# Two token groups with one gathered and one dense block in each, first gathers issued with the second mixer, and U products in four-pass float32

## The chip, the cores and the metric

The kernel runs on one core of a Trainium2 chip. The metric is the device time of one execution in microseconds, the median over executions. The core has five instruction streams that run side by side, each in its own order: TensorE (PE, with its weight loads PEld), VectorE (DVE), ScalarE (ACT), GpSimd (POOL) and SyncE (SP). SP issues the plain table loads, POOL the indirect ones, ACT some stores; the transfers themselves are carried by 16 DMA engines.

## The reference

One decoder block over 512 tokens of 1,024 features, float32, with 16 learned meta tokens in front. A mixer with two branches (8 heads of stick-breaking attention, 4 heads of gated linear attention) comes first, then a layer of 16,384 single-neuron experts. Each token looks up 128 of them, 16 for each of 8 heads, by the largest sums of two key scores:

```python
    s1 = jnp.einsum('thd,hkd->thk', q[:, :, 0], sub_keys1).astype(jnp.float32)
    s2 = jnp.einsum('thd,hkd->thk', q[:, :, 1], sub_keys2).astype(jnp.float32)
    v1, i1 = lax.top_k(s1, PEER_TOPK)
    v2, i2 = lax.top_k(s2, PEER_TOPK)
    cand = (v1[..., :, None] + v2[..., None, :]).reshape(T, PEER_HEADS, PEER_TOPK * PEER_TOPK)
```

The layer's output for a token is the sum over its 128 experts of softmax gate x gelu(x . U[e]) x V[e], where U and V are tables of 16,384 rows of 1,024 values (64 MiB each). It is added to the residual, and a last norm follows.

## The kernel before

The 512 tokens are four blocks of 128. `GROUPS = ((0, 1, 2), (3,))` makes two token groups. `front(g)` runs both mixer branches for a group (the second attends to the keys and values of the first too), `mid(g)` the output projection, the residual, the second norm and the expert queries. `proj` streams weights in chunks of 256 columns and multiplies them with the group's tokens, in one of two ways: *split*, where `hilo` makes a high and a low part of each operand and `mm3` (lines 185 to 189) multiplies three pairs of parts in one pass each; or *native*, one float32 product that the engine works off in four passes (two instructions in the trace). `topk(blk)` is a block's lookup, on VectorE almost alone: first the key scores, then the 16 largest, then tables.

Blocks in `DENSE` (0, 1, 2) compute **all** experts densely. For each of 128 groups of 128 experts (first key i1), `u_phase(i1)` loads a tile `uf` of the U table, splits it on ACT and VectorE (`uh`, `ul`) and makes 24 split passes of 384 token columns; gelu goes into a ring of 24 tiles. `v_operands(i1)` loads `vf`, splits it, and multiplies the ring tile with the dense weights `gt`; `v_block` adds 18 passes of 512 columns into six PSUM banks. `LA` = 23: U runs 23 groups ahead of V. The dense weights come from `spread(blk)`: for four tokens at a time it forms two one-hot operands (`B` on VectorE, `Am` on GpSimd, line 861), multiplies them (`px`, line 865) and stores the result to `Gd` in DRAM.

The block in `GATHER` (3) fetches its own rows. `gather` (line 807) is an indirect DMA on GpSimd's queue: one row of U or V for each of 128 tokens, 512 KB, into one of `GB` = 5 buffers `gu`. `u_dot` makes a dot product with it on VectorE (line 814, x in `xn`), `v_sum` adds a weighted V row to `y` (line 825), in a fixed order. So 128 + 128 gathers and as many VectorE operations serve a block.

The order of all this is the order in which Python issues it, refined by a scheduler that keeps each engine's queue in order. `SCHED` is a list written by hand for the second group: pieces of its mixer (f), middle (m), lookups (t, c) and spreads (s) of blocks 0 to 2 between them, and three early U products. Block 3's lookup and its gathers go into the dense stage, `TRATE` and `GRATE` steps per expert group.

Of the kernel before, what the change touches and what calls it, by code (L numbers as in the profile page):

```python
# [31 lines left out]
# PSUM banks for the key scores of the four blocks  # L32
SCT = ("px", "pz", "pz", "px")
# [30 lines left out]
NATIVE_PQ = (False, True)  # L64


def build(tc, d, out):
# [14 lines left out]

    wp = pool_open("wts", "wts0", side="right")
# [4 lines left out]
    # PSUM banks: 8 = pj 2, pz 3, po 3 (first group); pj 2, pk 2, pz 2, px 2 (second group); pj 2, acc 6  # L88
    nbuf = dict(pz=3, po=3)
# [17 lines left out]
    Gd = drp.tile([TB, 128, 128, TT], F32, name="Gd")  # L107
    hd = drp.tile([4, 128, D], F32, name="hd")

# [26 lines left out]
    def consts_b():  # L136
        nc.sync.dma_start(wgu, d["wgu"])
        nc.sync.dma_start(bgu, d["bgu"])
        lvf = pp.tile([128, 8, 128], F32, name="kT0")
# [19 lines left out]
    def rstd(ss, n, np_, pool, tag):  # L159
        """(ss / D + eps) ** -0.5 of sums of squares [np_, n]: exp(-ln / 2) and one Newton step."""  # L160
# [68 lines left out]
    def front(g):  # L229
        """Both mixer branches for the query blocks of group g; the meta tokens go with group 0."""  # L230
# [8 lines left out]
        oTh = (pp if g == 0 else wp).tile([128, KT, W], F32 if nato else F32R, name=f"oT{g}h")  # L239
        oTl = None if nato else pp.tile([128, KT, W], F32R, name=f"oT{g}l")  # L240
# [4 lines left out]
        kT = (pp if g == 0 else ap).tile([128, 4, W], F32, name=f"kT{g}")  # L245
        vt = (pp if g == 0 else ap).tile([128, nb, 512], F32, name=f"v{g}")
# [14 lines left out]
        def columns(x, rows, col, q):  # L261
            """A quarter of the features of normalised rows as columns of hn."""
# [26 lines left out]
        def rows_(c, vtile, mtile):  # L289
            """A chunk of values: tokens on partitions."""  # L290
            banks, outs, jobs = token_jobs(nb, NM, pm_)
            if g == 0:
                pm = banks[-1][:66, 256:]
                jobs.append((pm, 't', 0, 256, 0, 66, False))
# [25 lines left out]
        def gla_scores():  # L320
# [59 lines left out]
            for l in range(8):  # L380
                level(l)

        def gla_values():
            for c in range(2):
                cs = slice(c * 256, (c + 1) * 256)
                rows_(8 + c, gv[:, :, cs], gvm[:, cs] if g == 0 else None)

        def gla_out():
# [34 lines left out]
            for b, blk in enumerate(blks):  # L423
# [11 lines left out]
                if blk < 3:  # L435
                    state(NM + b * 128, 128, gv[:, b], False)

        def gla_silu():
            for c in range(2):
                for m, p in enumerate(feat(10 + c, NM)):  # L440
# [4 lines left out]
                    V.tensor_tensor(gr[:, 2 * c + m], p, e, op=OP.mult)  # L445

        def gla_norm():
            np_ = 2 if 2 * W <= 512 else 1
            n = np_ * W
            for s in range(2):  # L450
                for pr0 in range(0, 2, np_):
# [7 lines left out]
                    for j in range(np_):  # L459
# [6 lines left out]
                        else:  # L466
                            V.tensor_mul(rr[:, c_], rr[:, c_], gr[:, hh])
                            hilo(oTh[:, 4 + hh], oTl[:, 4 + hh], rr[:, c_])

        def sb_proj():  # L470
# [652 lines left out]
```

## Time and profile before

| what | value |
|---|---|
| three runs | 1712.67, 1713.15, 1717.16 us; median 1713.15 |
| profiled execution | span 1712.3 us |
| busy, share of the span | PE 95%, DVE 72%, ACT 41%, POOL 31% |
| DMA | 376.04 MB, mean 220 GB/s over the span |
| chain that ended last, by engine | PE 77%, DVE 14%, DMA 4%, ACT 2% |

The profiled execution's span is the stretch from its first to its last instruction; the runs are timed around it. A busy share is a mean over stages with different limits: the program runs through the first mixer group, lookups and second mixer, then the dense stage.

### The profile page before, as it was taken

How to read it: one execution, taken by the hardware profiler on the slowest of the kernel's cores; microseconds unless marked ns; L12 is line 12 of the kernel's file. 1: busy time of each engine (PE TensorE's matmuls, PEld its weight loads, DVE VectorE, ACT ScalarE, POOL GpSimd, SP SyncE). 2: the span in 40 equal slices, each digit the busy share in tenths (PEclk: the TensorE clock that was granted, in tenths of full speed). 3: DMA queues.
4: the chain of work that ended last, by engine and by line, in shares of the span. 5: the costliest groups of instructions: out<-in, count | busy, mean ns of one | idle time of the engine just before them, and what ended most of it. 6: DMA issues, size and time to landing. Idle time of an engine off the chain costs nothing.

```text
span 1712.3 us, 24535 instructions
## 1 busy us (share of the span) xinstructions
PE 1625.8 (95%) x9025; PEld 1448.6 (85%) x9025; DVE 1230.3 (72%) x2484; ACT 703.9 (41%) x1104; POOL 529.2 (31%) x401
## 2 busy tenths in 40 slices
PE   6999998988888799999999999999999999999996
PEld 5967988976678788989999999999999999999885
DVE  4225737389989998988777777777777777777674
ACT  5357355324455566333333333333333333333343
POOL 0020000002455565045434344343344443434310
PEclk9989999999999899999999999999999999999998
DMA  5210215243254345689887887887888887877653
GB/s 173 82 38 28 96 63 191 82 153 111 99 195 187 136 177 214 201 271 375 322 301 280 301 320 281 315 299 277 309 304 295 303 302 293 307 278 281 213 200 134
DMA packets 145705, 376.04 MB, mean 220 GB/s; under 512 B 13712, under 2 KB 63008, under 8 KB 142512
## 3 DMA queue, kind: packets, MB, share of 16 engines
q1 hardware_dynamic: 104112, 211.92, 36.2%
q0 software_dynamic: 36864, 134.23, 21.2%
q10 hardware_dynamic: 4608, 28.31, 4.1%
q8 instruction: 71, 1.16, 0.3%
q14 instruction: 50, 0.41, 0.1%
HBM read 345.03 MB, written 29.36 MB: 219 GB/s over the span
## 4 chain that ended last, share of the span: by engine, by line
PE 77%; DVE 14%; DMA 4%; ACT 2%; issue 1%; POOL 1%; SPq 0%; DVEq 0%; ACTq 0%; POOLq 0%
PE pj L189 12%; PE pj L187 12%; PE pj L188 12%; PE acc L188 9%; PE acc L189 9%; PE acc L187 9%; PE pk L209 3%; DVE B L859 2%; PE px L865 2%; PE pz L522 1%; PE pz L373 1%; PE pz L530 1%; DVE sc L775 1%; DMA gu<-expert_u,idx 1%; DMA vf<-expert_v 1%
## 5 line engine op out<-in xcount | busy, mean ns | idle before, releaser
L189 PE MATMUL pj<-xDh,ul 128*128 128x384 f32 x1000 | 337.3, 337 | 2.5 <-DVE ul L183 2.5
L187 PE MATMUL pj<-xDh,uh 128*128 128x384 f32 x1000 | 336.6, 337 | 0.0
L188 PE MATMUL pj<-xDl,uh 128*128 128x384 f32 x1000 | 336.2, 336 | 0.0
L188 PE MATMUL acc<-vl,wh 128*128 128x512 f32 x762 | 298.8, 392 | 2.8 <-DVE vl L183 2.8
L189 PE MATMUL acc<-vh,wl 128*128 128x512 f32 x762 | 298.6, 392 | 0.0
L187 PE MATMUL acc<-vh,wh 128*128 128x512 f32 x762 | 296.2, 389 | 0.0
L807 POOL DMA_INDIRECT gu<-expert_u,idx x128 | 189.4, 1479 | 324.2 <-DVE gu L814 183.7
L807 POOL DMA_INDIRECT gu<-expert_v,idx x128 | 178.7, 1396 | 277.2 <-DVE y L825 201.5
L182 ACT ACTIVATE uh<-uf 128x1024 fp32r<-128x1024 f32 x125 | 132.5, 1060 | 304.0 <-PE pj L188 262.4
L183 DVE TENSOR_TENSOR ul<-uf,uh 128x1024 fp32r<-128x1024 f32 x125 | 157.3, 1258 | 56.1 <-ACT uh L182 56.1
L187 PEld LDWEIGHTS pj<-xDh,uh 128*128 128x128 f32 x1000 | 188.3, 188 | 4.2
L188 PEld LDWEIGHTS pj<-xDl,uh 128*128 128x128 f32 x1000 | 188.2, 188 | 4.0
L189 PEld LDWEIGHTS pj<-xDh,ul 128*128 128x128 f32 x1000 | 188.2, 188 | 3.9 <-DVE ul L183 3.5
L188 PEld LDWEIGHTS acc<-vl,wh 128*128 128x128 f32 x762 | 143.0, 188 | 32.2 <-DVE vl L183 4.3
L189 PEld LDWEIGHTS acc<-vh,wl 128*128 128x128 f32 x762 | 143.0, 188 | 29.8
L187 PEld LDWEIGHTS acc<-vh,wh 128*128 128x128 f32 x762 | 143.1, 188 | 27.8 <-ACT vh L182 0.4
L825 DVE SCALAR_TENSOR_TENSOR y<-gu,act,y 128x1024 f32<-128x1024 f32 x128 | 163.9, 1280 | 0.5
L183 DVE TENSOR_TENSOR vl<-vf,vh 128x1024 fp32r<-128x1024 f32 x127 | 155.1, 1221 | 10.2 <-ACT vh L182 10.2
L861 POOL TENSOR_TENSOR Am<-ohu,ohl 128x512 f32<-128x512 f32 x96 | 132.6, 1399 | 95.3 <-PE px L865 57.8
L814 DVE SCALAR_TENSOR_TENSOR gu<-gu,xn 128x1024 f32<-128x1024 f32 x128 | 154.7, 1219 | 8.1 <-DMA gu<-expert_u,idx 8.1
L182 ACT ACTIVATE vh<-vf 128x1024 fp32r<-128x1024 f32 x127 | 133.0, 1047 | 16.7 <-DMA vf<-expert_v 14.4
L865 PE MATMUL px<-Am,B 128*128 128x128 f32 x768 | 105.5, 289 | 24.8 <-DVE B L859 13.2
(365 smaller groups left out, 2507.9 us busy)
## 6 DMA issues: line engine op xcount, KB each, us to landing
vf<-expert_v SPq DMA_DIRECT2D x128, 512.0 KB, 3.7
uf<-expert_ut SPq DMA_DIRECT2D x125, 512.0 KB, 5.0
wf<-w_in SPq DMA_DIRECT2D x48, 512.0 KB, 3.7
Gd<-st ACTq DMA_DIRECT2D x24, 1024.0 KB, 4.0
gt<-Gd SPq DMA_DIRECT2D x16, 1536.0 KB, 12.4
wf<-w_out SPq DMA_DIRECT2D x16, 512.0 KB, 3.7
wf<-w_pq SPq DMA_DIRECT2D x16, 512.0 KB, 3.7
h<-x SPq DMA_DIRECT2D x4, 512.0 KB, 6.5
```

The source lines that it names most:

```text
L182: A.activation(hi, src, AF.Copy)
L183: V.tensor_tensor(lo, src, hi.bitcast(F32), op=OP.subtract)
L187: T.matmul(outp, lh, rh, start=first, stop=False, skip_group_check=True)
L188: T.matmul(outp, lh, rl, start=False, stop=False, skip_group_check=True)
L189: T.matmul(outp, ll, rh, start=False, stop=last, skip_group_check=True)
L209: T.matmul(o, l, r, start=st, stop=sp, skip_group_check=True)
L807: P.indirect_dma_start(out=u, out_offset=None, in_=d[table], in_offset=bass.IndirectOffsetOnAxis(ap=col, axis=0))
L814: V.scalar_tensor_tensor(u, u, 1.0, xns[blk], op0=OP.mult, op1=OP.mult, accum_out=acts[blk][:, k:k + 1]))
L825: V.scalar_tensor_tensor(y, u, acts[blk][:, k:k + 1], y, op0=OP.mult, op1=OP.add))
L859: V.tensor_tensor(B, io4, iT[:, 1, c_].unsqueeze(2).to_broadcast(sh), op=OP.is_equal)
L861: P.tensor_tensor(Am.rearrange("p t (u l) -> p t u l", l=8), ohu[:, l_].unsqueeze(3).to_broadcast([128, 4, 16, 8]), ohl[:, l_].unsqueeze(2 ...
L865: T.matmul(p[:, j * 128:(j + 1) * 128], B[:, j], Am[:, j], start=True, stop=True)
```

## The change

The token groups become two of two blocks. In each the first block (0, 2) gathers and the second (1, 3) runs densely, so 512 gathers are issued instead of 256, and each dense product has 256 token columns instead of 384. Expert groups are taken in 64 pairs: one PSUM bank holds both groups' U results. U products are native float32 straight from the loaded tile `uf`, with no split; V products are native in every second pair (`V_NATIVE`) and split in the others. `Gd` has another layout (runs of 512 B in its writes, 8 KB in its reads).

The hand-written list goes. Every piece is now a generator that yields its estimated cost, and `weave(main, rate)` issues `rate` times that cost in background steps after each piece of a main sequence. The background has two queues: `look` (lookups and spreads) and `rows` (the gathered blocks' steps); `MIX` weighs them. The lookup of block 0 is issued whole right after the second group's first norm; then come `front(1)` and `mid(1)` with block 0's first gathers and the lookup of block 1; then 19 U pairs ahead of V with the lookup of block 3 and both spreads; then the dense loop with the lookup of block 2 and the other gathers; what is left is issued behind it. The core of the diff, without the many `yield` lines added to the mixer pieces:

```diff
+SCT = ("pz", "px", "px", "px")
...
-GROUPS = ((0, 1, 2), (3,))
-DENSE = (0, 1, 2)
-GATHER = (3,)
+GROUPS = ((0, 1), (2, 3))
+DENSE = (1, 3)
+GATHER = (0, 2)
 ND = len(DENSE)
+DT = ND * 128
 TT = 16
-TB = ND * 128 // TT
+TB = DT // TT
 IC = 8
-# float32 products as four passes (True) or as three passes over operands split in two (False), per token group
+NPAIR = NK // 2
...
+V_NATIVE = lambda p: p % 2 == 1
+RATES = (0.75, 1.0, 0.55)
+MIX = 0.4
+LA = 19
...
-    Gd = drp.tile([TB, 128, 128, TT], F32, name="Gd")
+    Gd = drp.tile([NK // IC, 128, TB, TT * IC], F32, name="Gd")
...
-            st = bp.tile([128, 128, TT], F32, name="st", bufs=2)
+            st = bp.tile([128, NK // IC, TT, IC], F32, name="st", bufs=2)
...
+            nc.scalar.dma_start(Gd[:, :, 128 // TT * DENSE.index(blk) + tb].rearrange("g p x -> p g x"),
+                                st.rearrange("p g t l -> p g (t l)"))
...
+    def gathered(blk):
+        for k in range(NK):
+            u_dot(blk, k)
+            yield 1.3
+        weights(blk, slice(0, NK))
+        y = gb.tile([128, D], F32, name=f"y{blk}")
+        ys[blk] = y
+        nc.sync.dma_start(y, hd[blk])
+        for k in range(NK):
+            v_sum(blk, y, k)
+            yield 1.3
...
+    def step(queue):
+        while queue:
+            c = next(queue[0], None)
+            if c is not None:
+                return c
+            queue.pop(0)
+        return None
+    mixed = [0.0]
+    def background():
+        if look and (not rows or mixed[0] < 1.0):
+            c = step(look)
+            if c is not None:
+                mixed[0] += MIX
+                return c
+        mixed[0] -= 1.0
+        return step(rows)
+    owed = [0.0]
+    def weave(main, rate):
+        for cost in main:
+            owed[0] += cost * rate
+            while owed[0] > 0:
+                c = background()
+                if c is None:
+                    owed[0] = 0.0
+                    break
+                owed[0] -= c
+    def finish(queue):
+        while step(queue) is not None:
+            pass
...
+    tks = {b: topk(b) for b in range(4)}
+    next(tks[0])
     pool_close("wts")
-    mp = pool_open("mid", "mid", side="right")
+    pool_close("ps")
+    gb = ctx.enter_context(tc.tile_pool(name="gat", bufs=1, reuse_waits="tile"))
+    wp = pool_open("wts", "wts1", side="right")
+    ps = pool_open("ps", "psb1", space=PSUM)
+    f1 = front(1)
+    next(f1)
+    for _ in range(1000):
+        if next(tks[0], None) is None:
+            break
+    rows.append(gathered(0))
+    look.append(tks[1])
+    weave(f1, RATES[0])
+    weave(mid(1), RATES[0])
+    finish(look)
...
+    def u_pair(p_):
+        ge = ring[p_] = du.tile([128, 2, DT], F32, name="ge", bufs=LA + 1)
+        pu = pj()
+        for i in range(2):
             uf = du.tile([128, KT, 128], F32, name="uf", bufs=2)
...
+            nc.sync.dma_start(uf, d["expert_ut"][2 * p_ + i])
+            for kt in range(KT):
+                T.matmul(pu[:, i * DT:(i + 1) * DT], uf[:, kt], xg[:, kt, :, 1, :], start=kt == 0, stop=kt == KT - 1)
+        A.activation(ge.rearrange("p a t -> p (a t)"), pu, AF.Gelu)
+    def ahead(n):
+        for p_ in range(n):
+            u_pair(p_)
+            yield 7.0
+    look.extend([tks[3], spread(1, 3), spread(3, 3)])
+    weave(ahead(LA), RATES[1])
+    finish(look)
+    look.append(tks[2])
...
+    def v_operands(p_):
         nonlocal gt
...
+        ge = ring.pop(p_)
+        vs = []
+        for i in range(2):
+            vf = dp.tile([128, D], F32, name="vf", bufs=3)
+            nc.sync.dma_start(vf, d["expert_v"][(2 * p_ + i) * 128:(2 * p_ + i + 1) * 128, :])
+            vs.append(vf)
+        if 2 * p_ % IC == 0:
+            gt = dp.tile([128, DT, IC], F32, name="gt", bufs=2)
+            nc.sync.dma_start(gt.rearrange("p t l -> p (t l)"), Gd[2 * p_ // IC].rearrange("p a x -> p (a x)"))
+        o = 2 * p_ % IC
+        V.tensor_tensor(ge, ge, gt[:, :, o:o + 2].rearrange("p t l -> p l t"), op=OP.mult)
+        if V_NATIVE(p_):
+            return ge, vs
+        wh = dp.tile([128, 2, DT], F32R, name="wh", bufs=2)
+        wl = dp.tile([128, 2, DT], F32R, name="wl", bufs=2)
+        hilo(wh, wl, ge)
+        hl = []
+        for vf in vs:
             vh = dp.tile([128, D], F32R, name="vh", bufs=2)
             vl = dp.tile([128, D], F32R, name="vl", bufs=2)
...
+            hilo(vh, vl, vf)
+            hl.append((vh, vl))
+        return (wh, wl), hl
+    def v_pair(p_, ops, ijs):
+        w, vs = ops
+        for e in range(2):
+            first, last = p_ == 0 and e == 0, p_ == NPAIR - 1 and e == 1
+            for i, j in ijs:
+                ts, ds_ = slice(i * 128, (i + 1) * 128), slice(j * 512, (j + 1) * 512)
+                if V_NATIVE(p_):
+                    T.matmul(acc[i][j], w[:, e, ts], vs[e][:, ds_], start=first, stop=last, skip_group_check=True)
+                else:
+                    mm3(acc[i][j], (w[0][:, e, ts], w[1][:, e, ts]), (vs[e][0][:, ds_], vs[e][1][:, ds_]), first, last)
+    ALL = [(i, j) for i in range(ND) for j in range(2)]
+    def dense():
+        started = False
+        for p_ in range(NPAIR):
+            if p_ + LA < NPAIR:
+                u_pair(p_ + LA)
+            ops = v_operands(p_)
+            if p_ < NPAIR - 1:
+                v_pair(p_, ops, ALL)
+            else:
+                for ij in ALL:
+                    v_pair(p_, ops, [ij])
+            if not look and not started:
+                started = True
+                rows.append(gathered(2))
+            yield 13.0 if p_ + LA < NPAIR else 6.0
+    weave(dense(), RATES[2])
+    finish(look)
+    finish(rows)
```

**GpSimd's queue.** Rows give operation, output, inputs and shape; `gu` is a gather buffer, `RS` the attention's running sum, `Am` the spread's one-hot operand. Before, from the second mixer to the first gathers:

```order
L543 COPY RS<-sp 128x512 x2
L861 TENSOR_TENSOR Am<-ohu,ohl 128x512 x5
L545 TENSOR_TENSOR RS<-RS,sp 128x512 x2
L861 TENSOR_TENSOR Am<-ohu,ohl 128x512 x2
L545 TENSOR_TENSOR RS<-RS,sp 128x512 x2
L861 TENSOR_TENSOR Am<-ohu,ohl 128x512 x3
L545 TENSOR_TENSOR RS<-RS,sp 128x512 x2
L861 TENSOR_TENSOR Am<-ohu,ohl 128x512 x86
L807 DMA gu<-expert_u,idx_6703 128x1024 x32
```

After, from the middle of the second mixer's attention to the end (the gather's line is now 811, the running sum's 566, `Am`'s 867; idx_2409 is block 0, idx_6101 block 2):

```order
L811 DMA gu<-expert_u,idx_2409 128x1024 x4
L566 TENSOR_TENSOR RS<-RS,sp 128x512
L811 DMA gu<-expert_u,idx_2409 128x1024 x2
L566 TENSOR_TENSOR RS<-RS,sp 128x512
L811 DMA gu<-expert_u,idx_2409 128x1024 x39
L867 TENSOR_TENSOR Am<-ohu,ohl 128x512 x64
L811 DMA gu<-expert_u,idx_2409 128x1024 x20
L811 DMA gu<-expert_v,idx_2409 128x1024 x128
L811 DMA gu<-expert_u,idx_6101 128x1024 x128
L811 DMA gu<-expert_v,idx_6101 128x1024 x128
```

The running sums of the second mixer's attention, which TensorE waits for, now stand between gathers of block 0; no gather stands between the 64 `Am` products of the two spreads.

**VectorE's queue, end of the dense stage.** `vl` is the split of a V tile, `wl` that of its weights, `gu,act` a dot product of `u_dot`, `y` a sum of `v_sum`, `acc` an accumulator bank. Before, near the end:

```order
L183 TENSOR_TENSOR vl<-vf,vh 128x1024
L183 TENSOR_TENSOR wl_14127<-oT0l,wh_14126 128x384
L825 SCALAR_TENSOR_TENSOR y<-gu,act_93,y 128x1024
L183 TENSOR_TENSOR vl<-vf,vh 128x1024
L825 SCALAR_TENSOR_TENSOR y<-gu,act_93,y 128x1024
L183 TENSOR_TENSOR wl_14162<-oT0l,wh_14161 128x384
```

After, from the last split of a V tile on (the dot product's line is now 818, the sum's 829; act_100 is block 2's):

```order
L194 TENSOR_TENSOR vl<-vf,vh 128x1024
L818 SCALAR_TENSOR_TENSOR gu,act_100<-gu,xn_3874 128x1024 x8
L1060 TENSOR_TENSOR vf<-acc_4086,vf 128x512
L818 SCALAR_TENSOR_TENSOR gu,act_100<-gu,xn_3874 128x1024
L1060 TENSOR_TENSOR vf<-acc_4087,vf 128x512
L818 SCALAR_TENSOR_TENSOR gu,act_100<-gu,xn_3874 128x1024 x3
L1060 TENSOR_TENSOR vf<-acc_4088,vf 128x512
L818 SCALAR_TENSOR_TENSOR gu,act_100<-gu,xn_3874 128x1024
L1060 TENSOR_TENSOR vf<-acc_4089,vf 128x512
L818 SCALAR_TENSOR_TENSOR gu,act_100<-gu,xn_3874 128x1024 x7
L823 TENSOR_TENSOR act_100<-act_100,gate_5589 128x128
L829 SCALAR_TENSOR_TENSOR y_9385<-gu,act_100,y_9385 128x1024 x128
```

The last sums of the gathered block stood among the splits of the dense stage; now the last 20 dot products and all 128 sums of block 2 stand behind the last split.

## Rows read from the trace of the kernel before

**Rows 1.** The page, busy times by engine: us, share, instructions

```profile
PE 1625.8 (95%) x9025; PEld 1448.6 (85%) x9025; DVE 1230.3 (72%) x2484; ACT 703.9 (41%) x1104; POOL 529.2 (31%) x401
```

**Rows 2.** Windows: length, busy PE, PEld, DVE, ACT, POOL, clock, DMA share, GB/s

```profile
27.00:88.00 61.00, 61.00 (x398) 58.86 (x397) 13.47 (x14) 19.87 (x37) 0.00 (x0) 0.98 0.29 99
88.00:202.00 114.00, 113.37 (x670) 83.97 (x670) 61.95 (x112) 63.20 (x113) 15.11 (x26) 0.97 0.14 48
202.00:287.00 85.00, 82.53 (x597) 74.41 (x595) 39.55 (x69) 43.52 (x85) 0.62 (x2) 1.00 0.32 111
287.00:338.00 51.00, 47.26 (x284) 46.16 (x284) 20.50 (x35) 21.57 (x50) 0.00 (x0) 0.93 0.29 103
338.00:741.00 403.00, 356.34 (x2282) 317.32 (x2283) 372.22 (x1292) 194.20 (x281) 142.98 (x105) 0.96 0.45 161
760.00:840.00 80.00, 80.00 (x405) 72.70 (x404) 66.78 (x104) 28.00 (x39) 35.73 (x24) 1.00 1.00 363
840.00:1570.00 730.00, 730.00 (x3693) 664.64 (x3692) 538.65 (x668) 257.43 (x359) 290.65 (x207) 1.00 0.83 297
1698.00:1713.00 15.00, 0.31 (x2) 0.00 (x0) 6.46 (x16) 1.74 (x6) 0.00 (x0) 0.66 0.42 140
```

**Rows 3.** Timeline of TensorE in the dense stage: start, duration, instruction

```profile
1003.88 0.33 PE L187 MATMUL pj<-xDh,uh 128*128 128x384 f32 x1
...
1008.07 0.39 PE L187 MATMUL acc<-vh,wh 128*128 128x512 f32 x1
...
1012.19 0.33 PE L187 MATMUL pj<-xDh,uh 128*128 128x384 f32 x1
```

**Rows 4.** Timeline of TensorE, native products of 256, 512 and 128 columns

```profile
506.25 3.72 PE L209 MATMUL pk<-wf,oT1h 128*128 128x256 f32 x16 [1.61 <-DMA wf<-w_out]
509.81 1.95 PE L865 MATMUL px<-Am,B 128*128 128x128 f32 x16
...
106.05 1.02 PE L530 MATMUL pz<-sp,cf 128*128 128x512 f32 x2
106.91 0.61 PE L537 MATMUL pz<-RS,cf 128*128 128x128 f32 x4
```

**Rows 5.** Timeline of VectorE: two steps of a lookup, the first dot product

```profile
338.02 0.87 DVE L730 MAX8 vv<-sc 128x8 f32<-128x128 f32 x4 [0.61 <-ACT sc L718]
...
392.97 3.60 DVE L779 TENSOR_REDUCE sel<-sc 128x128 f32<-128x2048 f32 x1
...
756.56 1.22 DVE L814 SCALAR_TENSOR_TENSOR gu<-gu,xn 128x1024 f32<-128x1024 f32 x1 [8.15 <-DMA gu<-expert_u,idx]
```

**Rows 6.** Timelines of GpSimd and VectorE: two gathers, and a split

```profile
752.22 0.94 POOL L807 DMA_INDIRECT gu<-expert_u,idx  x1 [0.30 <-issue]
...
790.25 1.22 DVE L183 TENSOR_TENSOR ul<-uf,uh 128x1024 fp32r<-128x1024 f32 x1
...
790.61 1.68 POOL L807 DMA_INDIRECT gu<-expert_u,idx  x1 [0.60 <-DVE gu L814]
```

**Rows 7.** Groups of instructions by line: busy, mean ns, idle before, releasers

```profile
L825 DVE SCALAR_TENSOR_TENSOR y<-gu,act,y 128x1024 f32<-128x1024 f32 x128 | 163.9, 1280 | 0.5
...
L861 POOL TENSOR_TENSOR Am<-ohu,ohl 128x512 f32<-128x512 f32 x96 | 132.6, 1399 | 95.3 <-PE px L865 57.8 <-DVE ohl L853 22.3 <-issue 10.7
...
L545 POOL TENSOR_TENSOR RS<-RS,sp 128x512 f32<-128x512 f32 x6 | 8.9, 1483 | 17.0 <-PE pz L534 10.2 <-issue 5.8 <-DVE tv L749 1.0
```

**Rows 8.** DMA from 760 to 840 us: GB/s by slice, issues with median landing

```profile
GB/s 356 307 396 400 389 377 324 335 298 375 398 416 403 418 408 401 408 406 389 387 350 383 334 354 406 350 339 323 322 409 403 416 397 389 354 346 55 354 371 277
...
vf<-expert_v SPq DMA_DIRECT2D x11, 512.0 KB, 7.0
uf<-expert_ut SPq DMA_DIRECT2D x11, 512.0 KB, 7.3
...
gu<-expert_u,idx POOLq DMA_INDIRECT x24, 8.2
```

More of the change, by code (lines that the diff above doesn't have):

```diff
@@ L81, in pool_close @@
         stk.pop(key).__exit__(None, None, None)
+    mp = pool_open("mid", "mid", side="right")
+    kv = pool_open("kv", "kv", side="right")
     wp = pool_open("wts", "wts0", side="right")
@@ L138, in consts_b @@
         nc.sync.dma_start(bgu, d["bgu"])
-        lvf = pp.tile([128, 8, 128], F32, name="kT0")
+        lvf = kv.tile([128, 8, 128], F32, name="kT0")
         nc.sync.dma_start(lvf, d["c_lvl"])
@@ L634, in mid @@
         if g == 0:
-            two = [pj(), pj(), po(), po()]
-            one = [po(), pz()]
+            banks = [pj(), pj(), px(), px()]
             for half in range(2):
                 for c in range(4):
-                    jobs = [(two[c][:, b * 256:(b + 1) * 256], 't', 0, 256, b * 128, (b + 1) * 128, b == 0)
+                    jobs = [(banks[c][:, b * 256:(b + 1) * 256], 't', 0, 256, b * 128, (b + 1) * 128, b == 0)
                             for b in range(2)]
-                    jobs.append((one[c // 2][:, c % 2 * 256:(c % 2 + 1) * 256], 't', 0, 256, 256, 384, c % 2 == 0))
                     proj(d["w_out"], c, jobs, oact, nato, halves=(half,))
+                    yield 3.0
             for c in range(4):
-                hs = h[:, :2, c * 256:(c + 1) * 256]
-                V.tensor_add(hs, two[c].rearrange("p (b c) -> p b c", b=2), hs)
-            for c in range(2):
-                hs = h[:, 2, c * 512:(c + 1) * 512]
-                V.tensor_add(hs, one[c], hs)
+                hs = h[:, :, c * 256:(c + 1) * 256]
+                V.tensor_add(hs, banks[c].rearrange("p (b c) -> p b c", b=2), hs)
         else:
@@ L653, in mid @@
                 proj(d["w_out"], c, jobs, oact, nato)
-                hs = h[:, 0, c * 256:(c + 1) * 256]
-                V.tensor_add(hs, outs[0], hs)
-        if g == 0:
-            xTh, xTl = pers["xDh"], pers["xDl"]
-        else:
-            xTh, xTl = wp.tile([128, KT, W], F32, name=f"oT{g}h"), None
+                hs = h[:, :, c * 256:(c + 1) * 256]
+                V.tensor_add(hs, banks[0].rearrange("p (b c) -> p b c", b=2), hs)
+                yield 7.0
         for b, blk in enumerate(blks):
@@ L882, in build @@
-    wp = pool_open("wts", "wts1", side="right")
-    pool_close("ps")
-    ps = pool_open("ps", "psb1", space=PSUM)
-    nbuf.update(pz=2, px=2, pk=2)
-    f1, m1 = front(1), mid(1)
-    tks = {b: topk(b) for b in range(4)}
-    ring = []
-    rblk = []
-    for nm, n in (("oT0h", 8), ("v0", 4), ("kT0", 4), ("oT0l", 8)):
-        rblk.append((len(ring), n, nm))
-        ring += [None] * n
-    LA = len(ring) - 1
-    acc = gt = dp = None
-    uname = {}
-    def ring_tile(i):
-        for o, n, nm in rblk:
-            if i == o and ring[i] is None:
-                t = pp.tile([128, n, ND * 128], F32, name=nm)
-                ring[o:o + n] = [t[:, j] for j in range(n)]
-                uname[o] = t
-        return ring[i]
@@ L925, in build @@
-    early = 0
-    for st in SCHED.split():
-        if st == "f":
-            next(f1, None)
-        elif st == "m":
-            next(m1)
-        elif st[0] == "c":
-            next(tks[int(st[1])])
-        elif st[0] == "t":
-            for _ in tks[int(st[1])]:
-                pass
-        elif st[0] == "u":
-            for _ in range(int(st[1:])):
-                u_phase(early, True)
-                early += 1
-        else:
-            tags = itertools.cycle(("px", "pk") if st[0] == "S" else ("px",))
-            spread(int(st[1]), bp, lambda: bank(next(tags)), 3)
@@ new lines, in build @@
+    gb = ctx.enter_context(tc.tile_pool(name="gat", bufs=1, reuse_waits="tile"))
[11 more added lines that the diff above has]
+    finish(look)
+    pool_close("wts")
+    pool_close("kv")
+    pool_close("ps")
+    pd = ctx.enter_context(tc.tile_pool(name="psd", bufs=1, space=PSUM, reuse_waits="tile"))
@@ L1032, in build @@
-    for _ in gen:
-        pass
-    for i in range(ND):
-        for j in range(2):
-            for i1 in sorted(last):
-                v_block(i1, i, last[i1], (j,))
+            hilo(vh, vl, vf)
[11 more added lines that the diff above has]
+                    mm3(acc[i][j], (w[0][:, e, ts], w[1][:, e, ts]), (vs[e][0][:, ds_], vs[e][1][:, ds_]), first, last)
@@ L1059, in build @@
     for i, blk in enumerate(DENSE):
-        hb = dp.tile([128, D], F32, name="vf", bufs=2)
+        hb = dp.tile([128, D], F32, name="vf", bufs=3)
         nc.sync.dma_start(hb, hd[blk])
         final(blk, hb, i)
+    pool_close("mid")
     ctx.close()
```

215 lines of the change are left out of this document (64 added, 151 removed).

## Prediction, made before the changed kernel was run

> **What bounds the kernel now.** I read the page's busy times first: TensorE is busy for 95% of the span, VectorE for 72% [rows 1]. The windows say where: from 840 to 1570 us TensorE is busy for 730 of 730 us at full clock, while the DMA engines are busy 0.83 of the time [rows 2]. There the order of instructions on TensorE gives the period: one group of 128 experts begins at 1003.88 us and the next at 1012.19, 8.31 us, of which 4.19 are the 24 U passes and 4.12 the 18 V passes [rows 3]. So a U pass of 384 columns takes 0.174 us, a V pass of 512 columns 0.229 (0.055 per 128 columns; 256 columns would take 0.119). Before 740 us the limits change: TensorE is busy for 356 of the 403 us from 338 on, and VectorE for 372 [rows 2]; that is where lookups, spreads and the second mixer share VectorE. The 256 gathers of block 3 hide fully in the dense stage. That stage sets the end.
>
> **What the change does to TensorE.** A product in float32 is two instructions of two passes each. Eight of 256 columns take 3.56 us from the first to the next product's start (506.25 to 509.81), 0.445 each; one of 512 columns takes 0.86 (106.05 to 106.91) [rows 4]; one of 128 about 0.22, a quarter of that. A pair of expert groups needs 16 U products: 16 x 0.445 = 7.1 us, for two dense blocks. V alternates: 24 split passes x 0.229 = 5.5 us or 8 native products x 0.86 = 6.9, on average 6.2. So a pair costs 13.3 us of TensorE where it cost 16.6, and 64 pairs 851 where they cost 1064. TensorE saves about 210 us there. The price is another 256 gathers. I sum stage by stage.
>
> **1, first group: 247 us.** It ends at VectorE's first search, now at 338.02 us [rows 5]. Its windows hold 61, 114, 85 and 51 us, all with a nearly full TensorE [rows 2]. With a third of the tokens gone: in the first, 192 feature passes x 0.055 and 48 value passes x 0.119, 16 us; in the second, half the attention columns (four passes of 512 columns, 22 fewer products x 0.86 = 19), 120 passes x 0.055, 48 x 0.119 and a third of the chunk scores, together 44; in the third, 96 x 0.055, 96 x 0.119 and some state work, 20; in the fourth, the query projection goes from 192 x 0.174 to 64 x 0.445 (minus 5) and a block of transposes goes, 10. One norm block less at the start: 1. 338 - 91 = 247.
>
> **2, lookup of block 0: 52.** Now it stands ahead of nearly everything of the second mixer on VectorE. Before, it ran from 338.02 to 396.6 (392.97 + 3.60) with other work in between [rows 5]; I take 58.6 less 13 for that work plus 6 for the norms. TensorE's two `pk` banks wait for VectorE meanwhile, so nothing covers it.
>
> **3, second mixer with the first gathers: 295 (255 to 350).** TensorE: 20 weight chunks x 16 x 0.445 = 142, attention over 7,168 columns 50, scores and the rest 36, 228 in all. VectorE: 103 dot products at 1.2 (the one at 756.56 took 1.22 [rows 5]) = 124, lookup of block 1 46, mixer 60, 230 in all. Two engines in order with equal work and mutual waits: 255 is the least. GpSimd decides above that. A gather occupies it 0.94 us when VectorE is idle, with 0.30 before the next (752.22), but 1.68 beside a busy VectorE, and 0.60 before the next when it waits for a buffer (790.61) [rows 6]. I take 1.7 for a gather, the value at which a VectorE busy three quarters of the time slows it. The last 92 gathers (156 us) and the running-sum adds queued between them (8 of 1.48 us [rows 7], others shorter: 24) make 180, behind a first part of 115. That part holds the wait for the first landing, 8.15 us on VectorE [rows 5], with the lookup and the chunk scores queued behind it.
>
> **4, 19 U pairs, lookup of block 3, spreads: 200.** TensorE: 19 x 7.1 = 135, spreads 64 x 4 x 0.22 = 57, scores 4. GpSimd's 64 products x 1.40 = 90 [rows 7] lie beside it. The order holds no gather here, so DMA idles.
>
> **5, dense: 768 (717 to 870).** TensorE alone: 45 x 7.1 + 64 x 6.2 = 717. Per pair with U, DMA moves four tables (2.1 MB), a quarter of a weight tile (0.26) and, at rate 0.55, 5.5 gathers (2.9 MB): 5.2 MB in 13.3 us, 394 GB/s. In 760 to 840 the DMA engines were busy all the time and moved 363 [rows 2], in its slices without many small packets about 400 [rows 8]. So 12.9 to 14.4 us per pair; I take 14.2, nearer the mean of a whole window. The first 10 pairs carry the lookup of block 2 and no gathers: 13.4. The last 19 have V only; the three `vf` tiles are held by native products while a load takes 7.0 us under load [rows 8], so 7.2 instead of 6.2. 134 + 497 + 137.
>
> By the Trainium skill's DMA: Bandwidth & Descriptors, Specifications, a core's share of HBM is about 358 GB/s. By that the 35 pairs would take 14.6 us, an estimate, and the stage 14 us more. The trace goes above it: slices of 400 and more [rows 8].
>
> **6, what is left of the gathers: 240 (179 to 325).** Behind the last `vl` the new VectorE order holds 20 dot products and 128 sums of block 2, and the split tiles are double, so VectorE can't run ahead of TensorE by more than some 12 us. 148 x 1.7 = 252, less 12. TensorE has nothing to do. VectorE alone would need 1.28 each [rows 7], so GpSimd leads. Both ends of the price: 1.29 us if only bytes count (0.52 MB at 405 GB/s), 2.28 if each gather waits for its buffer beside a busy VectorE (1.68 + 0.60 [rows 6]).
>
> **7, end: 13.** Before 15 [rows 2], with one block less.
>
> 247 + 52 + 295 + 200 + 768 + 240 + 13 = 1815 us of span. The profiled span is 1712.3, the timed median 1713.15, 0.85 more: **1816**. Most of the gain on TensorE survives, but the gathers come back at both ends of the dense stage: too few run before 800 us, and 148 stand bare behind it.
>
> **Rivals.**
>
> *Only bytes limit the gathers (the other side).* Place: dense stage and tail. If GpSimd isn't slowed beside VectorE, a gather takes 1.24 us there and DMA sets 1.29: tail 148 x 1.29 - 12 = 179; dense at TensorE's 717; the second mixer 280. 247 + 52 + 280 + 200 + 717 + 179 + 13 = 1688, faster. It decides from a sum of dense stage and tail below 906 us in that case; I have 1008. For it: slices above 400 GB/s, and 0.94 us in the undisturbed gathers. Against it: 1.68 us wherever VectorE is busy [rows 6], and VectorE is busy throughout the tail.
>
> The Trainium skill's SBUF — State Buffer, Who interferes with whom, holds that a VectorE operation with two SBUF inputs holds up only a GpSimd instruction that reads SBUF, and infers that descriptor generation needs the write side. By that rule the gathers would stay at 0.94 and this rival would hold. The trace disagrees: the split beside the gather at 790.61 has two SBUF inputs, and the gather took 1.68 [rows 6].
>
> *Each gather waits its turn.* At 2.28 us per gather: tail 148 x 2.28 - 12 = 325; in the second mixer 92 x 2.28 + 24 + 115 = 350; the dense stage hides it (5.5 x 2.28 = 12.5 per pair). 1955. For it: most gathers of before wait for VectorE. Against it: there VectorE's order spread them out; in the tail five buffers give 8.5 us for a round trip at 1.7, and a landing takes 8.2 even under load [rows 8].
>
> *U waits for its loads.* `uf` now goes straight into the products, in two tiles. The second is free at the end of a U and needed half a U after the next V begins its successor: 13.3 - 3.6 = 9.8 us. The load takes 7.3 [rows 8], so by the rows it costs nothing; with five gathers always queued beside it, 12 us would cost 45 x 2.2 = 99 us: 1915.
>
> **How the numbers follow.** Forecast 0.62, bytes only 0.16 (0.12 of it faster, 0.04 landing within 0.3%, when only part of it holds), own turn 0.12, U loads 0.10. Within 0.3% (5 us) is about what a measurement of this kernel can't tell from no change. Faster 0.12, same 0.04, slower 0.84. The range leaves out the centre of the first rival and that of the second, and holds the third: 1710 to 1935. The forecast's own range is 1755 to 1880.
>
> **What would show it.** In the new profile: first search near 247 us; first gather near 300, and 16 us to its product; no gather between some 595 and 795 us; a period of 13.3 to 14.5 us per pair with DMA near 1.0; about 240 us at the end with TensorE idle and GpSimd's gathers at 1.7. I am wrong if the tail's gathers come at 1.3 us, if the dense stage keeps TensorE full with DMA above 390 GB/s, or if the second mixer takes under 250 us.

## The result, and the profile after

The changed kernel takes 1975.47 us (median of 4, 1964.07 to 1979.94) against 1715.16: a ratio of 1.152, 95% interval 1.148 to 1.156. The profiled execution's span is 1974.3 us. The forecast was 1816 us, with a range to 1935: the sign was right, the size 159 us short.

The page of the changed kernel, busy times, then the span in 40 slices; they answer to [rows 1]:

```profile
PE 1464.9 (74%) x6570; PEld 1112.9 (56%) x6570; DVE 1229.5 (62%) x2400; ACT 388.6 (20%) x675; POOL 781.6 (40%) x619
...
PE   6999848977767999988998898888888899600000
...
POOL 0000002167454054502244444444444344577774
PEclk9899979988879999999999899999899899855555
DMA  5212415685587456676888888888888788888986
```

TensorE lost 161 us of work (1625.8 before), but no engine is near 95% any more. From the 23rd slice on TensorE is mostly at 8 tenths where the dense stage of before had it full [rows 2], while DMA is at 8 and not at 9; the last five slices hold gathers and their sums, with TensorE idle.

The windows are cut at the first search, the first gather, the first U product, the first V product, the last U product and the last V product (length, then busy time of PE, PEld, DVE, ACT, POOL, clock, DMA share, GB/s), as in [rows 2]:

```profile
0.00:255.00 255.00, 221.43 (x1446) 189.40 (x1446) 103.16 (x195) 111.85 (x219) 9.44 (x25) 0.97 0.33 107
255.00:301.00 46.00, 19.76 (x93) 14.16 (x93) 45.70 (x267) 12.03 (x35) 0.00 (x0) 0.70 0.20 61
301.00:634.00 333.00, 258.34 (x1123) 188.19 (x1123) 218.78 (x559) 78.83 (x152) 155.37 (x126) 0.90 0.70 240
634.00:866.00 232.00, 217.09 (x1257) 192.58 (x1255) 151.04 (x428) 61.89 (x100) 85.05 (x64) 1.00 0.59 180
866.00:1551.00 685.00, 603.80 (x2241) 442.44 (x2242) 424.85 (x629) 93.60 (x124) 283.16 (x210) 0.95 0.84 315
1551.00:1720.00 169.00, 144.37 (x416) 86.13 (x415) 96.50 (x143) 23.91 (x27) 73.31 (x58) 0.90 0.85 298
1720.00:1974.00 254.00, 0.11 (x1) 0.00 (x0) 189.44 (x183) 6.48 (x20) 175.32 (x137) 0.51 0.85 296
```

| stage | forecast | measured | off by |
|---|---|---|---|
| 1, first group | 247 | 255 | +8 |
| 2, lookup of block 0 | 52 | 46 | -6 |
| 3, second mixer | 295 | 333 | +38 |
| 4, U pairs ahead | 200 (+14) | 232 | +18 |
| 5, dense | 768 (-14) | 854 | +100 |
| 6, gathers left | 240 | 240 | 0 |
| 7, end | 13 | 14 | +1 |

The 14 in stages 4 and 5: 672 U instructions ran ahead of the first V product, 21 pairs and not 19 (32 instructions a pair), so 7.1 us for each of the two belong to stage 4. The dense stage holds 100 of the 159 us.

Inside it, the timeline of TensorE over one split and one native pair (compare [rows 3]):

```profile
1205.65 7.07 PE L976 MATMUL pj<-xall,uf 128*128 128x256 f32 x32
1212.55 7.03 PE L1025 MATMUL acc<-vf,ge 128*128 128x512 f32 x16
1220.99 3.69 PE L976 MATMUL pj<-xall,uf 128*128 128x256 f32 x16 [1.41 <-DMA uf<-expert_ut]
1226.85 3.72 PE L976 MATMUL pj<-xall,uf 128*128 128x256 f32 x16 [2.17 <-DMA uf<-expert_ut]
1230.22 0.58 PE L198 MATMUL acc<-vh,wh 128*128 128x512 f32 x1
```

U takes 6.9 us and native V 6.9, as worked out; the time is lost in front of U's tiles. From 1041.6 to 1528.7 us 961 U instructions ran, 30 pairs: 16.2 us each where I had 14.2. What SP's own queue waits for in that stretch (total us, times, longest):

```profile
SPq L998 <- DVE vl L194: 147.1, 30, 15.5
SPq L998 <- DMA vf<-expert_v: 96.7, 15, 8.6
SPq L1002 <- DVE ge L1004: 81.4, 7, 12.8
SPq L974 <- PE pj L976: 76.2, 26, 5.4
```

L998 is the load of a V tile. It waits for a free tile, above all one that VectorE's split `vl` has not yet released; the U loads (L974) come behind it in the same queue. The V loads of this stretch on SP's queue:

```profile
1190.93 0.89 SPq L998 DMA_DIRECT2D vf<-expert_v  x2
...
1212.94 0.33 SPq L998 DMA_DIRECT2D vf<-expert_v  x1
...
1221.88 0.33 SPq L998 DMA_DIRECT2D vf<-expert_v  x1
...
1222.78 0.86 SPq L998 DMA_DIRECT2D vf<-expert_v  x2
```

After 1191.8 one single V load went out until 1221.88, while the native pair computed until 1219.6. So the native pair seems to hold two of the three tiles, and the split pair has to pass both of its tiles through the third. That is read from the order of the rows; e2 and e10 test it. What follows each load stands in the timelines of ACT and VectorE, at the same place:

```profile
1219.55 1.06 ACT L193 ACTIVATE vh<-vf 128x1024 fp32r<-128x1024 f32 x1 [13.30 <-DMA vf<-expert_v]
```

```profile
1211.68 1.23 DVE L194 TENSOR_TENSOR vl<-vf,vh 128x1024 fp32r<-128x1024 f32 x1
...
1220.63 1.22 DVE L194 TENSOR_TENSOR vl<-vf,vh 128x1024 fp32r<-128x1024 f32 x1 [7.12 <-ACT vh L193]
1221.78 2.60 DVE L829 SCALAR_TENSOR_TENSOR y<-gu,act,y 128x1024 f32<-128x1024 f32 x2
```

The load at 1212.94 goes out as the first `vl` ends (1211.68 + 1.23). ACT waits 13.3 us for a V tile's data, VectorE 7.1 us for ACT, and the sums of gathered rows stand behind the second `vl`. So gather buffers aren't released either, gathers stop, and DMA idles (busy for 0.20 of the time from 1219.5 to 1224 us) while everybody waits for a load that was issued late.

### The profile page after: what moved, and what is told of

Read it like the earlier page. It is cut to its first block, busy times and chain, and to the rows that moved or that the text cites. A ratio compares the mean times of both kernels' runs of the same rounds, so it can differ in the third digit from the quotient of the medians.

```text
span 1974.3 us, 19216 instructions
## 1 busy us (share of the span) xinstructions
PE 1464.9 (74%) x6570; PEld 1112.9 (56%) x6570; DVE 1229.5 (62%) x2400; ACT 388.6 (20%) x675; POOL 781.6 (40%) x619
## 4 chain that ended last, share of the span: by engine, by line
issue 27%; PE 25%; DMA 23%; DVE 11%; POOL 10%; ACT 3%; DVEq 0%; POOLq 0%; SPq 0%; ACTq 0%
DMA gu<-expert_v,idx 10%; POOL gu L811 10%; PE pj L976 7%; DMA vf<-expert_v 4%; PE pk L220 3%; DMA gu<-expert_u,idx 3%; DMA wf<-w_in 3%; PE px L871 2%; DVE y L829 2%; DMA wf<-w_pq 2%; DVE ge L1004 2%; DMA uf<-expert_ut 1%; PE pz L543 1%; PE pz L551 1%; PE pz L386 1%
## 5 line engine op out<-in xcount | busy, mean ns | idle before, releaser
L811 POOL DMA_INDIRECT gu<-expert_u,idx x256 | 329.7, 1288 | 643.7 <-DVE gu L818 398.6
L976 PE MATMUL pj<-xall,uf 128*128 128x256 f32 x2048 | 489.7, 397 | 83.3 <-DMA uf<-expert_ut 66.0
L976 PEld LDWEIGHTS pj<-xall,uf 128*128 128x128 f32 x2048 | 402.9, 200 | 168.8 <-ACT vh L193 51.8
L811 POOL DMA_INDIRECT gu<-expert_v,idx x256 | 338.5, 1322 | 253.5 <-DVE y L829 172.6
L829 DVE SCALAR_TENSOR_TENSOR y<-gu,act,y 128x1024 f32<-128x1024 f32 x256 | 328.9, 1285 | 114.9 <-DMA gu<-expert_v,idx 107.1
L818 DVE SCALAR_TENSOR_TENSOR gu<-gu,xn 128x1024 f32<-128x1024 f32 x256 | 312.2, 1244 | 138.2 <-DMA gu<-expert_u,idx 136.9
L1025 PE MATMUL acc<-vf,ge 128*128 128x512 f32 x512 | 225.0, 592 | 0.0
L198 PE MATMUL acc<-vh,wh 128*128 128x512 f32 x256 | 114.1, 446 | 18.1 <-ACT vh L193 13.1
L199 PE MATMUL acc<-vl,wh 128*128 128x512 f32 x256 | 106.9, 418 | 11.4 <-DVE vl L194 11.4
L200 PE MATMUL acc<-vh,wl 128*128 128x512 f32 x256 | 105.4, 413 | 0.0
L871 PE MATMUL px<-Am,B 128*128 128x128 f32 x512 | 64.1, 280 | 7.9 <-DVE B L865 6.2
```

What stands on the lines that cost most here:

```text
L198: T.matmul(outp, lh, rh, start=first, stop=False, skip_group_check=True)
L199: T.matmul(outp, lh, rl, start=False, stop=False, skip_group_check=True)
L200: T.matmul(outp, ll, rh, start=False, stop=last, skip_group_check=True)
L811: P.indirect_dma_start(out=u, out_offset=None, in_=d[table], in_offset=bass.IndirectOffsetOnAxis(ap=col, axis=0))
L818: V.scalar_tensor_tensor(u, u, 1.0, xns[blk], op0=OP.mult, op1=OP.mult, accum_out=acts[blk][:, k:k + 1]))
L829: V.scalar_tensor_tensor(y, u, acts[blk][:, k:k + 1], y, op0=OP.mult, op1=OP.add))
```

## The experiments

e5, e6, e9, e10 and e13 edit the changed kernel as it is, with U 19 pairs ahead of V; the others have 15 pairs (e11 has 11), since their tiles need the space, and e2 to e4 are compared with e1. Times are medians. The period is 400 us over the U pairs (instructions / 32) that ran from 1000 to 1400 us; the tail is all that follows the end of the last V product, the end of some 14 us included.

| run | us | U pairs in 400 us | period | GB/s there | tail |
|---|---|---|---|---|---|
| changed kernel | 1975 | 24.9 | 16.1 | 328 | 254 |
| e1 | 1964 | 25.0 | 16.0 | 324 | 241 |
| e2, five V tiles | 1850 | 30.1 | 13.3 | 400 | 239 |
| e3, four U tiles | 1975 | 24.0 | 16.6 | 319 | 241 |
| e4, seven gather buffers | 1948 | 26.0 | 15.4 | 343 | 198 |
| e9, U loads on ACT | 1960 | 25.0 | 16.0 | 327 | 255 |
| e10, V all split | 1871 | 29.5 | 13.6 | 388 | 264 |
| e13, no gathers in the loop | 2189 | 30.4 | 13.1 | 179 | 577 |
| e14, e2 and V all split | 1848 | 29.9 | 13.4 | 392 | 243 |

Theory Q: a V load that waits for one of three tiles holds up SP's queue. Its rivals: two U tiles, DMA's bandwidth, and, for the tail, five gather buffers.

**e1 to e4.**

```diff
-LA = 19
+LA = 15
```

> The changed kernel with U only 15 pairs ahead of V instead of 19; it frees the space that the three kernels beside it use and is what they are compared with. Four U pairs (7.1 us each, 28) move from the stage ahead into the dense loop, where a pair with U takes 16.3 us and one without 8.6: all theories give 1965 to 1990 us.

```diff
-            vf = dp.tile([128, D], F32, name="vf", bufs=3)
+            vf = dp.tile([128, D], F32, name="vf", bufs=5)
```

> U 15 pairs ahead, five tiles for V loads instead of three. Theory Q (SP issues loads in order; a V load that waits for one of three tiles holds back the U loads queued behind it, and DMA idles): the pair period falls from 16.3 to between 13.5 and 14.7 us, DMA rises from 322 to 350 GB/s or more, the time falls by 60 to 100 us against three tiles. Rival U (two U tiles are the limit): under 25 us. Rival B (beside gathers DMA carries no more than some 320 GB/s): under 15 us, same GB/s.

```diff
-            uf = du.tile([128, KT, 128], F32, name="uf", bufs=2)
+            uf = du.tile([128, KT, 128], F32, name="uf", bufs=4)
```

> U 15 pairs ahead, four tiles for U loads instead of two. Rival U: the time falls by 60 to 100 us against two tiles. Theory Q: under 25 us, since U loads still stand behind the V load that waits. Rival B: under 15 us.

```diff
-GB = 5
+GB = 7
```

> U 15 pairs ahead, seven gather buffers instead of five. If GpSimd, slowed beside VectorE, sets the tail: 235 to 250 us behind the last V product as with five buffers. If the round trip through five buffers sets it: the period of 1.72 us per gather falls by up to 5/7 to 1.3, the tail to 180 to 210. In the dense stage theory Q expects no change of the pair period beyond 0.3 us; rival B none.

e1 changes little. Five V tiles take away 114 us, more than expected; four U tiles gain nothing (1975 against 1964). Windows of e2, all instructions, then those of the U products alone:

```profile
1000.00:1400.00 400.00, 397.88 (x1585) 299.59 (x1584) 282.15 (x294) 59.22 (x77) 206.30 (x166) 1.00 1.01 400
...
1000.00:1400.00 400.00, 212.79 (x963) 182.15 (x961) 1.00 1.01 400
```

and of e3 (all instructions):

```profile
1000.00:1400.00 400.00, 348.50 (x1261) 255.33 (x1259) 226.10 (x202) 43.24 (x60) 173.69 (x132) 0.91 0.85 319
```

With five tiles TensorE works 397.9 of 400 us, while DMA carries 400 GB/s with as many gathers as my forecast had (166 in 30 pairs). So rivals U and B fall: the bytes fit. e4 shortens the tail to 198 us (184 without the end, within what the round trip lets expect), which speaks against GpSimd as its only limit. Its period fell by 0.6 us where I expected no more than 0.3; that fits a chain that gathers are part of, through the sums that stand ahead of `vl`.

**e9 and e10, the tiles or the queue.**

```diff
-            nc.sync.dma_start(uf, d["expert_ut"][2 * p_ + i])
+            nc.scalar.dma_start(uf, d["expert_ut"][2 * p_ + i])
```

> The changed kernel with U's loads issued by ACT instead of SP; buffers as they were (three V tiles, two U tiles, U 19 pairs ahead). If the order of SP's queue is the cause by itself (U loads held back by a V load that waits for a tile): the dense loop shortens by 40 to 90 us, 1885 to 1935. If the V loads themselves, with three tiles, set the period: within 20 us of 1975. If ACT, waiting for U tiles in order, holds back its splits and gelu: slower than 1990.

```diff
-V_NATIVE = lambda p: p % 2 == 1
+V_NATIVE = lambda p: False
```

> The changed kernel with V split in every pair, three V tiles. If the native pairs' hold on V tiles (until their last product) sets the period: tiles come free after VectorE's split, TensorE needs 5.5 instead of 6.9 us in half of the pairs, the dense loop and the V-only pairs shorten by 60 to 120 us: 1855 to 1915. If VectorE's additional 64 splits (78 us) and their waits among the gathers' products are as bad: 1950 to 2000.

U's loads on ACT's queue gain 16 us, under 1%. That doesn't refute theory Q, for ACT's queue holds them back too, behind a split that waits for the same V tile; e9's timeline of ACT:

```profile
1210.69 1.06 ACT L193 ACTIVATE vh<-vf 128x1024 fp32r<-128x1024 f32 x1 [13.32 <-DMA vf<-expert_v]
1210.77 0.82 ACTq L974 DMA_DIRECT2D uf<-expert_ut  x2
```

The two U loads went out at 1210.77 us, though the U products that had held their tiles had ended by 1203.9. So how much of the wait the queue's order makes stays open. What is shown is its root, the V loads with three tiles: five tiles take the wait away (e2), and splitting every V tile, so that no native product holds one, gains 104 us (e10). Windows of e10:

```profile
1000.00:1400.00 400.00, 378.60 (x1664) 318.38 (x1663) 319.23 (x318) 97.41 (x121) 223.57 (x164) 0.98 1.00 388
```

In e10 DMA is full and TensorE is not.

**e13 and e14, what makes three tiles too few.** e13 holds back all gathers until the loop is issued:

```diff
-            if not look and not started:
-                started = True
-                rows.append(gathered(2))
             yield 13.0 if p_ + LA < NPAIR else 6.0
...
+    held = rows[:]
+    rows.clear()
     weave(dense(), RATES[2])
     finish(look)
+    rows.extend(held + [gathered(2)])
```

> The changed kernel with all remaining gathers issued behind the dense loop (three V tiles; VectorE's order then has none of their products ahead of 48 of its 64 V splits). If the native products' hold on three tiles is enough by itself: the period per pair with U stays at 15 us or more. If it takes the gathers beside it (longer loads, VectorE's queue): 13.2 to 13.8 us with TensorE nearly full. The total by either: some 380 gathers behind the loop at 1.7, 2150 to 2300 us.

> Five V tiles, U 15 pairs ahead, V split in every pair. If both remove the same wait: the U part of the dense loop gets only TensorE's difference (12.6 instead of 13.3 us a pair) or is held by bytes at 375 GB/s: 1815 to 1850 us. If each removes its own: 1760 to 1800.

Windows of e13, and the DMA views from 1000 to 1250 us (count, size, median us to landing) of e13, then of e14:

```profile
1000.00:1400.00 400.00, 400.00 (x1598) 302.26 (x1597) 83.79 (x78) 61.44 (x78) 0.00 (x0) 1.00 0.58 179
```

```profile
uf<-expert_ut SPq DMA_DIRECT2D x39, 512.0 KB, 3.7
vf<-expert_v SPq DMA_DIRECT2D x38, 512.0 KB, 3.7
```

```profile
uf<-expert_ut SPq DMA_DIRECT2D x38, 512.0 KB, 7.8
vf<-expert_v SPq DMA_DIRECT2D x37, 512.0 KB, 6.7
```

Without gathers three tiles do: TensorE is full, and a load lands in 3.7 us where one beside gathers and a full DMA takes 6.7 to 7.8 (e14). So it takes both, tiles held by native products and gathers beside the loads. Whether the longer load or VectorE's queue does more isn't separated. e14 gains nothing over e2: both edits remove the same wait, and then DMA is full (392 GB/s, share 1.01).

**e5, the tail.**

```diff
-            V.scalar_tensor_tensor(y, u, acts[blk][:, k:k + 1], y, op0=OP.mult, op1=OP.add))
+            V.scalar_tensor_tensor(y[:, :8], u[:, :8], acts[blk][:, k:k + 1], y[:, :8], op0=OP.mult, op1=OP.add))
```

> The changed kernel with each weighted sum of a gathered V row cut to 8 of its 1,024 columns (the gathers stay, the rest of the sum is left out), so that VectorE is nearly idle behind the last V product. Theory G (GpSimd's gather is slowed beside VectorE): a gather takes 0.94 us and the period falls from 1.72 to the 1.25 to 1.35 that bytes allow; the tail falls from 243 to 175 to 195. Rival L (the round trip through five buffers): only the 1.28 us of the sum leave a round trip of 5 x 1.72 = 8.6, so 1.45 to 1.6 a gather and a tail of 210 to 230.

Groups of instructions of e5 behind the last V product (busy, mean ns of one, idle before it):

```profile
L811 POOL DMA_INDIRECT gu<-expert_v,idx x128 | 122.4, 957 | 50.2 <-issue 37.9 <-DVE y L829 12.3
L829 DVE SCALAR_TENSOR_TENSOR y<-gu,act,y 128x8 f32<-128x8 f32 x124 | 28.1, 226 | 138.3 <-DMA gu<-expert_v,idx 138.3
```

of the changed kernel, from 1730 to 1950 us:

```profile
L811 POOL DMA_INDIRECT gu<-expert_v,idx x127 | 163.0, 1283 | 50.5 <-issue 28.0 <-DVE y L829 14.1 <-DMA gu<-expert_v,idx 8.4
```

and of e4:

```profile
L829 DVE SCALAR_TENSOR_TENSOR y<-gu,act,y 128x1024 f32<-128x1024 f32 x125 | 160.6, 1285 | 17.1 <-DMA gu<-expert_v,idx 11.8 <-issue 0.9 <-DVE y L829 0.6
L811 POOL DMA_INDIRECT gu<-expert_v,idx x120 | 136.3, 1136 | 37.5 <-issue 35.0 <-DVE y L829 1.2 <-DMA gu<-expert_v,idx 0.9
```

In the changed kernel the period is (163.0 + 50.5) / 127 = 1.68 us, of which the gather takes 1.283. With VectorE nearly idle (e5) a gather takes 0.957 us and the period is (122.4 + 50.2) / 128 = 1.35, as theory G has it; the tail is 210 us, 196 without the end, at the edge of G's figure and short of L's. But with seven buffers, and VectorE busier (0.89 of the time from 1750 to 1941 us), the period is (136.3 + 37.5) / 120 = 1.45, the gather 1.14. So 1.68 takes both: a gather slowed beside VectorE, and a round trip through only five buffers. The two shares aren't separated: e5's shorter sum also shortens the round trip, and in both runs DMA was near full (0.99 in e5 from 1705 to 1885 us, 0.96 in e4).

**e6, e7, e8, e11 and e12, where gathers are cheap.** e6 appends block 0's gathers after `mid(1)`, and it and e7 set `mixed[0] = 0.0` ahead of `weave(ahead(LA), ...)`, which lets gathers into that stage (e7 in e2's kernel); e8 and e12 change e2's rates, e11 adds `GB = 7` to e2 with `LA = 11`:

```diff
-RATES = (0.75, 1.0, 0.55)
+RATES = (0.75, 1.0, 0.85)
...
+RATES = (1.3, 1.0, 0.75)
```

> The changed kernel with block 0's gathers issued only from the stage ahead of the dense loop on. If the gathers lengthen the second mixer (weight loads wait beside them, VectorE's dot products stand in the way): from 333 us between first gather and first U product to 235 to 270, counted from the end of block 0's lookup. If TensorE's own work and mutual waits set it: 300 or more. The total: some 28 of the 103 gathers go into the stage ahead, the other 60 to 75 end up behind the last V product at 1.72 each (208 there instead of 148), so 1980 to 2020 us by the first, 2050 to 2090 by the second.

> Five V tiles, U 15 pairs ahead, and gathers let into the stage ahead of the dense loop, where DMA was busy for 0.60 (23 more gathers there, some 15 more with the lookup's end, 115 behind the last V product instead of 148). If a gather is free there: that stage grows by under 10 us and the tail falls by 33 x 1.6 = 53: 1785 to 1810 us. If GpSimd's one-hot products or VectorE's queue set that stage: it grows by 30 to 50 and nothing is gained, 1835 to 1860.

> Five V tiles, U 15 pairs ahead, background rate in the dense loop 0.85 instead of 0.55: all gathers are issued within the dense loop, none behind it. If DMA sets the dense loop (0.96 busy, 375 GB/s with five tiles): the 148 gathers (78 MB) cost 78 / 0.375 = 208 us there instead of 240 behind it, 1800 to 1835 us. If the gathers hide in the loop: 1610 to 1680. If VectorE's order makes new waits there: 1850 or more.

> Five V tiles and seven gather buffers, U 11 pairs ahead (all that the space allows). If the two effects add (dense loop 110 us shorter by the V tiles, tail 35 us shorter by the buffers): 1805 to 1830 us. If more gathers in flight take DMA from the table loads: 1840 to 1880.

> Five V tiles, U 15 pairs ahead, background rates 1.3 beside the second mixer (some 70 more gathers there, which cost 46 us for 103) and 0.75 in the dense loop (nothing left behind it). If the rest is limited by bytes (318 MB at 365 GB/s after some 570 us): 1745 to 1800 us. If VectorE becomes the bound beside the mixer (219 + 90 us of work in a stage of 335): that stage grows by 60 or more and the gain is lost, 1810 to 1850.

The second mixer in e6 and in e12 (windows, first gather or search's end to the first U product):

```profile
302.00:588.00 286.00, 248.95 (x1119) 183.72 (x1116) 91.37 (x351) 78.33 (x152) 20.67 (x23) 0.92 0.28 91
```

```profile
301.00:747.00 446.00, 274.70 (x1118) 199.21 (x1116) 328.89 (x669) 92.42 (x162) 254.87 (x212) 0.79 0.80 278
```

e6 took 2067 us. Without gathers the mixer still takes 286, between the two expectations; the time is the second's, with a tail of 374. So 103 gathers cost 47 us there, 0.46 each. e12 (1878 us, slower than e2) shows that the next ones aren't so cheap: 86 more, by the count on GpSimd (212 against 126), lengthen e2's stage of 322 by 124, 1.4 each, with VectorE busy 329 of 446 us; the gain was lost, more fully than expected. e7 (1832) gained 19 on e2, 9 between the profiled spans: the tail fell by 42, the second mixer and the stage ahead grew by 33. Windows of e8 (1822), and what its V loads waited for from 1000 to 1400 us:

```profile
854.00:1687.00 833.00, 659.45 (x2401) 483.67 (x2402) 613.05 (x845) 101.99 (x136) 464.57 (x361) 0.89 0.95 361
```

```profile
SPq L998 <- DVE vl L194: 151.9, 22, 18.7
```

Its tail is gone, and the dense stage is 202 us longer than e2's (960 against 758), as the case "DMA sets the dense loop" has it. That bytes are the limit isn't shown by it: DMA moved 361 GB/s where e2 had carried 400, and the V loads waited for `vl` again. e11 took 1909 us, 58 more than e2 with a tail 54 shorter: the effects don't add. In its loop DMA moved 364 GB/s from 1000 to 1400 us, and U waited for its loads again (46.8 us up to 1450); four fewer U pairs ahead are in it too, so the buffers' share isn't known. None of these versions beats the kernel before.

## Why the prediction was wrong

- **Direction, and where the gathers go: right.** TensorE's saving came (161 us less work over all), its prices too: U 6.9 us a pair against 7.1, native V 6.9. What is left of the gathers took 240 us, the forecast to the microsecond. That is in part luck: I had GpSimd lead with gathers of 1.7 us, five buffers being enough, and the period of 1.68 came from gathers of 1.28 and 0.40 between them. e4 and e5 each shorten the tail, so it takes both. "Bytes only" (1.29) and "own turn" (2.28) are out as centres.
- **The step that failed: stage 5**, "I take 14.2", which let DMA's bytes set the period. They don't: e2 carries 400 GB/s over 400 us, above the 363 that I leaned on. Three V tiles beside gathers set 16.2. I had seen the tiles ("the three `vf` tiles are held by native products while a load takes 7.0 us under load") and priced them at 1 us in the last 19 pairs only. From 1554 us on 20 pairs with V only took 166 us, 8.3 each where I had 7.2, 22 more; the 30 pairs with U took 16.2 for 14.2, 60 more; the other 17 or so of the 100 lie elsewhere in the stage. Not all of it is idle time: the clock was 0.94 in the 30 pairs and 0.90 with V only, where it had been 1.00 before [rows 2]. That the term's upper end, 870, held 854 was luck; it wasn't put there for the V tiles.
- **The rival "U waits for its loads"** had the place where TensorE waits and named the wrong tile: four U tiles gain nothing (e3), five V tiles 114 us (e2). TensorE's wait shows at the end of the chain, in front of a U tile, and not at its start, the V tile. The first rival's mark, 906 us for dense stage and tail, goes with a second mixer of 295; with the rival's own 280 it is 920. The measured 854 + 240 is above both.
- **Stage 3, mis-sized by 38, on the wrong path.** I had GpSimd decide: 180 us of gathers and sums behind a first part of 115. GpSimd was busy for 155 of the 333 us, and without gathers (e6) the stage still has 286, so the mixer's own work and waits set most of it; the gathers add 47. Beside them weight loads hold TensorE for 34 us (`wf` loads of three tables: 14.5, 12.3 and 7.2 in the view of waits), in e6 for 7.6. The clock is 0.90 in it, 0.92 in e6.
- **Stage 4** is 18 longer: 512 spread instructions of 64.1 us in all (57 forecast) and 15 us in which TensorE waits.
- By the Trainium skill's DMA: Bandwidth & Descriptors, Specifications, some 358 GB/s is a core's share of HBM, and with that rule the loop would be 14.6 us a pair. e2's 400 GB/s over 400 us is above it; the loop was slower for another reason.
- The Trainium skill's SBUF — State Buffer, Who interferes with whom, would leave gathers at 0.94 us beside VectorE. e5 against the changed kernel (0.957 against 1.283 from 1730 to 1950 us) says no; the measurement decides.

The range failed because its upper end was a single rival on the forecast sum; stages 3, 4 and 5 all missed upwards, by 156 together. None of the three signs of being wrong that I had named came in the changed kernel: the failure was one that I hadn't listed.

## What to carry to other kernels

When an operand is used straight from its load tile, that tile is held until the last product, not until a copy is made: count the tiles again, with the load's time beside the other traffic (here some 7 us, not 3.7). Two edits that each bring 100 us may bring 100 together: look for the wait that both remove. Price a gather by stage: here it cost 0.46 us for the first 103 beside the second mixer, 1.4 for 86 more there, and 1.7 bare behind the dense loop.

## What the runs showed of the hardware

One core's DMA carried 400 GB/s over 400 us (e2). And in the tail, a gather waits for the end of the VectorE operation that runs when it begins; timelines of GpSimd and of VectorE in the changed kernel:

```profile
1800.53 1.86 POOL L811 DMA_INDIRECT gu<-expert_v,idx  x1 [1.17 <-DVE y L829]
1802.70 1.02 POOL L811 DMA_INDIRECT gu<-expert_v,idx  x1 [0.30 <-issue]
1804.02 1.02 POOL L811 DMA_INDIRECT gu<-expert_v,idx  x1 [0.30 <-issue]
```

```profile
1798.98 6.57 DVE L829 SCALAR_TENSOR_TENSOR y<-gu,act,y 128x1024 f32<-128x1024 f32 x5 [0.82 <-DMA gu<-expert_v,idx]
```

The five sums follow each other every 1.31 us; the second ends at 1801.58, the third at 1802.90, the fourth at 1804.22. The gathers that begin during these three end at 1802.39, 1803.72 and 1805.04, each 0.81 or 0.82 us behind the end of its sum, however long the sum had still to run. It is so throughout: from 1730 to 1950 us 107 of 131 gathers took over 0.97 us; each of them began while a VectorE operation ran and ended 0.81 us (to 0.01) after that operation did. In e4, from 1760 to 1930 us, the same holds for 116 of 117. The other 24 took 0.93 to 0.95: 19 began while VectorE was idle, five within 0.1 us of an operation's start or end. What VectorE and the gather share there, no run here shows.
